# Sums of squares and state-space tables on VectorE alone, table builds one feature tile later, in a hybrid decoder layer

## The chip, the cores and the metric

One Trainium2 chip, one of its cores. The metric is the device time of one execution in microseconds (us); a result is the median of several executions.

## What is computed

One decoder layer over 512 tokens with 2048 features, in float32. The input is normalised, projected to q, k, v and u, goes through attention (q, k, v) and a diagonal state-space model (u) side by side, then through an output projection, a gated MLP and a last norm. Cut to what matters here:

```python
hn = _rmsnorm(h, norm1_g)                       # needs the sum of squares of each token
q, k, v, u = split(hn @ w_in)
a_bar = exp(lam * dt)                           # 64 groups x 64 complex states
b_bar = ((a_bar - 1.0) / lam)[..., None] * b_mat
bu = einsum('bsgp,gnp->bsgn', u, b_bar)
states = associative_scan(a, a * x + bu)        # over the 512 positions
y = einsum('bsgn,gpn->bsgp', states, c_mat).real + d_skip * u
ssm_out = gelu(y) * sigmoid(gelu(y) @ w_glu + b_glu)
h = h + concat([attn_out, ssm_out]) @ w_out
h = h + (silu(n(h) @ w_gate) * (n(h) @ w_up)) @ w_down
```

## The kernel before

Activations are kept transposed: features on the 128 partitions, tokens on the free axis. The projections are done at float32 accuracy by three matmuls on TensorE (PE) for each 128x128 block of weights and 128x512 block of activations: high by high, high by low, low by high (`mm3`, L108 to L111). So each weight chunk of 512 KB that arrives by DMA is split (`split`, L89 to L91): ScalarE (ACT) copies it into the high part, `whi`, and VectorE (DVE) subtracts to get the low part, `wlo`. There are four raw chunks and five pairs of high and low halves. Each of the 16 tiles of x is split the same way when it arrives (`gsplit`, whose VectorE half is the instruction at L59).

The program text gives instructions in program order, and a scheduler that simulates the engines then sets the order on each engine. Every engine works its own list strictly in that order, so an instruction whose input is late holds up all that stand behind it on that engine.

The stages, in the order of the program:

- **The x phase** (L198 to L222): x arrives in 16 tiles, is split, and tiles 0 and 1 of u are computed together, as the tiles arrive: 192 matmuls.
- **Sums of squares** (L223 to L230): ScalarE squares each tile of x into `sq_x`, and 15 additions gather them in `ssacc`, all on GpSimd (POOL) at L229. `rstd_of` (L141 to L161) turns them into the factor of the norm by small matmuls (`ss`, L146).
- **Tables** (L236 to L357): the powers `pr`, `pi` of the state matrix are computed on VectorE in many small operations, and the discretised input matrix `bbr`, `bbi` by six operations of 128x1024 (L330 to L335), three of them on GpSimd.
- **The u loop** (L451 to L458): tiles 2 to 7 of u (96 matmuls each). Behind a tile two of the eight `ssm_build` calls follow (tiles 3 to 6), and two of the eight `ssm_local` calls (tiles 4 to 7, the last one behind the first tile of q).
- **`ssm_build`** (L379 to L418): `combine` (L367 to L375) forms the table `E` of 128x1024 out of `bbr`, `bbi` and the powers: two products and a sum, in two halves of 512 columns, the first half on VectorE, the second on GpSimd. `cc` and `cz` (L392 to L394) are three small operations on GpSimd. TensorE transposes E in eight pieces (`etp`, L401) and multiplies it by `cz` (`gps`, L406); a DMA round trip turns the result into the table `T`.
- **`ssm_local`** (L422 to L438): products `vps` (L430) of u with E, copied to `Xh`, and `lps` (L437) with T.
- **The recurrence** (L482 to L489): 62 steps of five small VectorE operations on `Xh`, beside the tiles of q and k.
- **`ssm_out`** (L502 to L525): eight calls behind the tiles 5 to 7 of k. Each loads its part of Xh (`xt`, L509), forms a table `w` by `combine`, multiplies (`yps`, L517), adds to U on VectorE, applies Gelu on ScalarE and stores it by eight DMAs that ScalarE's queue issues (`sy`, L523).
- v (L542 to L554), attention, the gate of the state-space output, the output projection, and the MLP, which takes the rest of the time from about 770 us on.

Of the kernel before, what the change touches and what calls it, by code (L numbers as in the profile page):

```python
# [15 lines left out]
ALU = mybir.AluOpType  # L16
# [10 lines left out]
T = 8  # L27
# [8 lines left out]
def _emit(tc, a, y):  # L36
    nc = tc.nc
    act, dve, pool, pe = nc.scalar, nc.vector, nc.gpsimd, nc.tensor
# [10 lines left out]
    def tt(out, in0, in1, op, eng=None):  # L49
        (eng or dve).tensor_tensor(out=out, in0=in0, in1=in1, op=op)  # L50
# [33 lines left out]
    def aux(shape, name):  # L84
        return psum.tile(shape, F32, tag="aux", name=name, bufs=3)
# [55 lines left out]
    def rstd_of(acc_t, out, name):  # L141

        n = acc_t.shape[-1] // 128
        ps = aux([128, 4], "ss_" + name)
        for m in range(n):
            pe.matmul(ps[:, m:m + 1], acc_t[:, 128 * m:128 * m + 128], ones[:, 0:1], start=True, stop=True)  # L146
        st = cpool.tile([128, 4, 4], F32, tag="rst", name="rst_" + name)
        v, q, r, c = (st[:, i, :n] for i in range(4))
        ts(v, ps[:, :n], 1.0 / D, EPS, ALU.mult, ALU.add)
        act.activation(q, v, AF.Sqrt)  # L150
        dve.reciprocal(r, q)
        stt(q, v, -0.5, r, ALU.mult, ALU.mult)
        tt(q, q, r, ALU.mult)
        stt(c, q, 1.5, r, ALU.add, ALU.mult)
        dg = wpool.tile([128, 4, 128], F32, tag="sq", name="dg_" + name, bufs=4)
        for m in range(n):
            ts(dg[:, m, :], ident, c[:, m:m + 1])
        bc = aux([128, 512], "bc_" + name)
        pe.matmul(bc[:, :128 * n], ones, dg[:, :n].rearrange("p m t -> p (m t)"), start=True, stop=True)
        act.activation(out, bc[:, :128 * n], AF.Copy)  # L160
        return c  # L161
# [13 lines left out]
    ssacc = cpool.tile([128, 512], F32, tag="ss", name="ssacc")  # L175
# [47 lines left out]
    for k in range(KT):  # L223
        if k == 0:
            act.activation(ssacc, xr[k], AF.Square)
        else:
            sq = wpool.tile([128, 512], F32, tag="sq", name=f"sq_x{k}", bufs=4)
            act.activation(sq, xr[k], AF.Square)
            tt(ssacc, ssacc, sq, ALU.add, pool)  # L229
    rsc = rstd_of(ssacc, rstd, "1")  # L230

    for t, n in ((g2, "g2"), (gf, "gf"), (bg, "bg")):
# [15 lines left out]
    brt = sa.tile([128, NG, 16], F32, tag="E", name="brt")  # L248
    bit = sa.tile([128, NG, 16], F32, tag="tm", name="bit")
# [4 lines left out]
    z, k_, r, ki = small(), small(), small(), small().bitcast(I32)  # L254
# [42 lines left out]
    for n in (1, 2, 4):  # L297
# [4 lines left out]
        t_ = pt[:, :, :n]  # L302
# [23 lines left out]
    bbi = sp.tile([128, NG, 16], F32, name="bbi")  # L326
    bt = sp.tile([128, NG, 16], F32, tag="T", name="bt", bufs=2)
    frb = fr.unsqueeze(2).to_broadcast([128, NG, 16])
    fib = fi.unsqueeze(2).to_broadcast([128, NG, 16])
    tt(bbr, brt, frb, ALU.mult)  # L330
    tt(bbi, bit, frb, ALU.mult, pool)
    tt(bt, bit, fib, ALU.mult)
    tt(brt, brt, fib, ALU.mult, pool)
    tt(bbr, bbr, bt, ALU.subtract)
    tt(bbi, bbi, brt, ALU.add, pool)  # L335


    low, high = slice(0, 64), slice(64, 128)
# [2 lines left out]
    q4 = sp.tile([128, 2, NG], F32, name="q4")  # L341
# [24 lines left out]

    def combine(dst, tmp, c_re, c_im, n0):  # L367

        for i, eng in enumerate((dve, pool)):
            gs = slice(4 * i, 4 * i + 4)  # L370
            w = [c[:, gs].unsqueeze(2).to_broadcast([128, 4, T, 16]) for c in (c_re, c_im)]
            p = [t_[:, gs, n0:n0 + T].unsqueeze(3).to_broadcast([128, 4, T, 16]) for t_ in tables]
            tt(dst[:, gs], w[0], p[0], ALU.mult, eng)
            tt(tmp[:, gs], w[1], p[1], ALU.mult, eng)
            tt(dst[:, gs], dst[:, gs], tmp[:, gs], ALU.add, eng)  # L375

    built = {}

    def ssm_build(b):  # L379
        nonlocal tables  # L380
        gs = slice(8 * b, 8 * b + 8)
        tables = PA[:, gs], PB[:, gs]
        E_ = sa.tile([128, 8, T, 16], F32, tag="E", name=f"E{b}")
        tmp = sa.tile([128, 8, T, 16], F32, tag="tm", name=f"Et{b}")
        combine(E_, tmp, bbr[:, gs], bbi[:, gs], 0)

        cz = sp.tile([128, 8, 2, 16], F32, tag="cz", name=f"cz{b}", bufs=1)
        cc = sp.tile([128, 2, 8, 16], F32, tag="cb", name=f"cb{b}", bufs=1)
        side.dma_start(cc, a["c_c"][b])
        for r, pp in enumerate((slice(0, 64), slice(64, 128))):  # L390
            side.dma_start(cz[pp, :, 0], a["c_c"][b][pp, r])
        for r in range(2):  # L392
            tt(cc[:, r], cc[:, r], q4[:, r, gs].unsqueeze(2).to_broadcast([128, 8, 16]), ALU.mult, pool)
        tt(cz[:, :, 1], cc[:, 0], cc[:, 1], ALU.add, pool)  # L394
        dsk = sp.tile([16, 16, 8], F32, tag="dsk", name=f"dsk{b}", bufs=2)
        side.dma_start(dsk, a["d_skip"][:, :, 8 * b:8 * b + 8])
        et = sp.tile([128, 8, 128], F32, tag="et", name=f"et{b}", bufs=2)
        for i in range(2):
            ps = aux([128, 4, 128], f"etp{b}_{i}")
            for q in range(4):  # L400
                pe.transpose(ps[:, q, :], E_[:, 4 * i + q].rearrange("p a b -> p (a b)"), ident)  # L401
            act.activation(et[:, 4 * i:4 * i + 4], ps, AF.Copy)

        gps = aux([64, 8, 32], f"gps{b}")
        for q in range(8):
            pe.matmul(gps[:, q, :], E_[:, q, 0:4, :].rearrange("p a b -> p (a b)"), cz[:, q].rearrange("p a b -> p (a b)"),  # L406
                      start=True, stop=True)
        G = sp.tile([64, 2, 16, 8], F32, tag="G", name=f"G{b}", bufs=2)
        for i in range(2):
            act.activation(G[:, i], gps[:, :, 16 * i:16 * i + 16].rearrange("p g q -> p q g"), AF.Copy)  # L410
        tt(G[0:16, 0], G[0:16, 0], dsk, ALU.add)
        g_ = gz[b % 2]
        side.dma_start(g_[112:240].rearrange("(i r) q g -> r i (q g)", i=2), G.rearrange("p i q g -> p i (q g)"))
        tm_ = sp.tile([128, T, 16, 8], F32, tag="T", name=f"T{b}", bufs=2)
        src = g_[0:128].rearrange("r q g -> r (q g)")
        src = bass.AP(tensor=src.tensor, offset=src.offset, ap=[[128, 128], [16 * 128, T], [1, 128]])
        side.dma_start(tm_.rearrange("r i q g -> r i (q g)"), src)
        built[b] = et, tm_  # L418

    tables = None  # L420

    def ssm_local(b):  # L422
        p0, p1 = 4 * b, 4 * b + 4
        et, tm_ = built.pop(b)

        vps = aux([128, 2, 4, 64], f"vps{b}")
        for ri in range(2):
            for q in range(4):
                for e in range(2):
                    pe.matmul(vps[64 * e:64 * e + 64, ri, q, :], et[:, 2 * q + e, 64 * ri:64 * ri + 64],  # L430
                              U[:, 8 * b + 2 * q + e, :], start=True, stop=True)
        for ri in range(2):
            dve.tensor_copy(Xh[:, ri, p0:p1, 1:64], vps[:, ri, :, 0:63])

        lps = aux([128, 8, 64], f"lps{b}")
        for g in range(8):
            pe.matmul(lps[:, g, :], tm_[:, :, :, g].rearrange("p i q -> p (i q)"), U[:, 8 * b + g, :], start=True, stop=True)  # L437
        act.activation(U[:, 8 * b:8 * b + 8, :], lps, AF.Copy)  # L438

    def u_out(f, ps):  # L440
        ut = wpool.tile([128, T, NC_], F32, tag="sq", name=f"ut{f}", bufs=4)
        tt(ut, ps.rearrange("p (c j) -> p j c", j=T), rstd.rearrange("p (c j) -> p j c", j=T), ALU.mult)
        su = tc.dram_tile([128, T, NC_], F32, name=f"su{f}")
        side.dma_start(su, ut)
        sv = su.rearrange("(g p) j c -> j p g c", p=16)
        for j in range(T):
            side.dma_start(U[16 * (7 - j):16 * (7 - j) + 16, 8 * f:8 * f + 8, :], sv[j])

    u_out(0, u01[0])
    u_out(1, u01[1])  # L450
    for f in range(2, 8):  # L451
        ps = acc(f"u{f}")
        ftile(ps, [a["w_u"][2 * f], a["w_u"][2 * f + 1]], xs, f"u{f}")
        u_out(f, ps)
        for b in {4: (0, 1), 5: (2, 3), 6: (4, 5), 7: (6,)}.get(f, ()):
            ssm_local(b)
        for b in {3: (0, 1), 4: (2, 3), 5: (4, 5), 6: (6, 7)}.get(f, ()):
            ssm_build(b)  # L458
    qpool = opened("q", bufs=1)
    rc = qpool.tile([32, 512], F32, name="rc")  # L460
    rs = qpool.tile([32, 512], F32, name="rs")
# [14 lines left out]
        return t_  # L476

    qs = [qk_tile("q", 0, qpool)]
    ssm_local(7)


    for c in range(1, 63):  # L482
# [75 lines left out]
    for b in range(8):  # L558
        yt = wpool.tile([128, 512], F32, tag="sq", name=f"yt{b}", bufs=4)
        nc.sync.dma_start(yt, sy[b].rearrange("p i c -> p (i c)"))  # L560
        t_ = laid(ring2, "B", f"ysp{b}", 8, 4)
# [23 lines left out]
    for h in range(NH):  # L585
# [4 lines left out]
        for step in "t0 t1 t2 p0 t3 p1 p2 p3".split():  # L590
            j = int(step[1])
            w = 512 - 128 * j
# [84 lines left out]
    for e in range(2):  # L677
        es = E[e]
        for f in range(KT):
# [9 lines left out]
            else:  # L689
                sq = wpool.tile([128, 512], F32, tag="sq", name=f"sq_h{e}_{f}", bufs=4)[:, 0:256]  # L690
# [112 lines left out]
    for p in range(NPH):  # L803
        ms = []
        for q in range(4):
            f = 4 * p + q
# [114 lines left out]
```

## Time and profile before

| | us |
|---|---|
| median of 3 runs | 2112.76 (2112.38 to 2114.86) |
| the profiled execution, its own time | 2112.28 |
| span of that execution in the profile | 2110.5 |
| TensorE busy | 2053.3 (97%) |
| VectorE busy | 1535.6 (73%) |
| ScalarE busy | 865.6 (41%) |
| GpSimd busy | 198.1 (9%) |
| mean granted TensorE clock | 0.986 |

The busy times are those of one execution. Its own time is 1.8 us over its span, since the span goes from the first to the last instruction. The mean clock is a share of full speed (2.4 GHz); the two levels that are granted are 1.2 and 2.4 GHz. Matmuls overlap, so the time from one start to the next says more about TensorE's pace than the duration of one.

### The profile page before, as it was taken

To read this page: it belongs to the slowest core of one execution; us is meant where nothing else is said; L and a number is where in the kernel's file an instruction comes from. 1 tells how busy PE (TensorE), PEld (TensorE's weight loads), DVE (VectorE), ACT (ScalarE), POOL (GpSimd) and SP (SyncE) were. 2 spreads that over 40 slices of the span, in tenths; PEclk is the share of its full clock that TensorE was granted. 3 is DMA by queue.
4 is the path that set the end of the run, shared out by engine and by line. 5 is a ranking of instruction groups with operands and counts; after the bars stand their busy time and mean duration, and the time that the engine had idled before them with its cause. 6 is when DMAs were issued, how large, how long until landed. Compare 5 with 4: busy or idle time off the path is not lost.

```text
span 2110.5 us, 35164 instructions
## 1 busy us (share of the span) xinstructions
PE 2053.3 (97%) x13522; PEld 1858.4 (88%) x13522; DVE 1535.6 (73%) x2932; ACT 865.6 (41%) x1523; POOL 198.1 (9%) x172
## 2 busy tenths in 40 slices
PE   7899999999999979999999999999999999999996
PEld 5688888877889979899998989899998989999896
DVE  8835897555436989687786968687686868778686
ACT  5222222346325645344443535344352535444354
POOL 4533102300002360000000000000000000000002
PEclk9999999999999989999999999999999999999998
DMA  6443234623324614323232223323232332323232
GB/s 222 127 121 112 92 102 140 178 81 125 125 91 169 206 65 140 121 100 120 82 129 90 101 101 120 111 90 130 85 124 83 111 110 101 120 88 124 90 121 80
DMA packets 117193, 244.24 MB, mean 116 GB/s; under 512 B 39040, under 2 KB 57312, under 8 KB 117024
## 3 DMA queue, kind: packets, MB, share of 16 engines
q1 hardware_dynamic: 107808, 239.88, 33.8%
q10 hardware_dynamic: 9216, 2.10, 0.5%
q8 instruction: 106, 1.74, 0.3%
q14 instruction: 63, 0.52, 0.1%
HBM read 229.77 MB, written 9.03 MB: 113 GB/s over the span
## 4 chain that ended last, share of the span: by engine, by line
PE 87%; DVE 7%; issue 2%; DMA 1%; ACT 1%; SPq 0%; POOL 0%; DVEq 0%; ACTq 0%; POOLq 0%
PE gu L109 12%; PE gu L111 12%; PE gu L110 12%; PE dn L110 7%; PE dn L109 7%; PE dn L111 7%; PE lps L437 1%; PE q L111 1%; PE q L110 1%; PE oa L111 1%; PE oa L109 1%; PE oa L110 1%; PE q L109 1%; PE v L550 1%; PE v L552 1%
## 5 line engine op out<-in xcount | busy, mean ns | idle before, releaser
L110 PE MATMUL dn<-m,whi_dn 128*128 128x512 f32 x640 | 249.0, 389 | 0.0
L109 PE MATMUL dn<-m,whi_dn 128*128 128x512 f32 x640 | 248.8, 389 | 0.0
L111 PE MATMUL dn<-m,wlo_dn 128*128 128x512 f32 x640 | 248.8, 389 | 0.0
L50 DVE TENSOR_TENSOR h<-h,dn 128x512 f32<-128x512 f32 x160 | 109.9, 687 | 172.5 <-PE dn L111 171.3
L90 ACT ACTIVATE whi_dn<-raw_dn 128x512 fp32r<-128x512 f32 x160 | 100.9, 632 | 240.5 <-PE dn L110 208.2
L50 DVE TENSOR_TENSOR raw_r<-raw_r,raw_r 128x512 f32<-128x512 f32 x264 | 182.5, 691 | 2.2
L111 PEld LDWEIGHTS dn<-m,wlo_dn 128*128 128x128 f32 x640 | 120.2, 188 | 24.9
L109 PEld LDWEIGHTS dn<-m,whi_dn 128*128 128x128 f32 x640 | 120.2, 188 | 24.6
L110 PEld LDWEIGHTS dn<-m,whi_dn 128*128 128x128 f32 x640 | 120.2, 188 | 24.5
L50 POOL TENSOR_TENSOR h<-h,ssf 128x256 f32<-128x256 f32 x12 | 10.7, 920 | 1300.1 <-ACT ssf L160 1300.1
L50 DVE TENSOR_TENSOR wlo_dn<-raw_dn,whi_dn 128x512 fp32r<-128x512 f32 x160 | 109.8, 687 | 17.6 <-ACT whi_dn L90 16.5
L109 PE MATMUL gu<-c,whi_C 128*128 128x256 f32 x352 | 99.8, 284 | 1.9 <-ACT c L90 1.6
L111 PE MATMUL gu<-c,wlo_E 128*128 128x256 f32 x352 | 98.8, 281 | 2.8 <-DVE wlo_E L50 2.8
L109 PE MATMUL gu<-c,whi_D 128*128 128x256 f32 x352 | 98.3, 279 | 2.7 <-ACT whi_D L90 2.7
L109 PE MATMUL gu<-c,whi_E 128*128 128x256 f32 x352 | 98.5, 280 | 2.4 <-ACT whi_G L90 1.7
L111 PE MATMUL gu<-c,wlo_D 128*128 128x256 f32 x352 | 98.5, 280 | 2.0 <-DVE wlo_D L50 2.0
L111 PE MATMUL gu<-c,wlo_C 128*128 128x256 f32 x352 | 99.5, 283 | 0.5 <-DVE wlo_C L50 0.5
L110 PE MATMUL gu<-c,whi_C 128*128 128x256 f32 x352 | 99.6, 283 | 0.1
L110 PE MATMUL gu<-c,whi_E 128*128 128x256 f32 x352 | 98.3, 279 | 0.0
L110 PE MATMUL gu<-c,whi_D 128*128 128x256 f32 x352 | 98.0, 278 | 0.0
L109 PE MATMUL gu<-c,whi_F 128*128 128x256 f32 x352 | 97.7, 277 | 0.0
L109 PE MATMUL gu<-c,whi_G 128*128 128x256 f32 x352 | 97.5, 277 | 0.2 <-ACT whi_G L90 0.2
(323 smaller groups left out, 6673.1 us busy)
## 6 DMA issues: line engine op xcount, KB each, us to landing
raw_r<-w_gu SPq DMA_DIRECT2D x176, 512.0 KB, 3.6
raw_dn<-w_down SPq DMA_DIRECT2D x80, 512.0 KB, 4.1
raw_os<-w_out SPq DMA_DIRECT2D x32, 512.0 KB, 3.4
raw_q<-w_q SPq DMA_DIRECT2D x16, 512.0 KB, 3.5
raw_k<-w_k SPq DMA_DIRECT2D x16, 512.0 KB, 3.4
raw_v<-w_v SPq DMA_DIRECT2D x16, 512.0 KB, 3.7
raw_oa<-w_out SPq DMA_DIRECT2D x16, 512.0 KB, 3.5
raw_u<-w_u SPq DMA_DIRECT2D x15, 512.0 KB, 4.7
```

What stands on the lines that cost most here:

```text
L50: (eng or dve).tensor_tensor(out=out, in0=in0, in1=in1, op=op)
L90: act.activation(hi, raw, AF.Copy)
L109: pe.matmul(ps, wh, x[:, 0, :], start=first, stop=False)
L110: pe.matmul(ps, wh, x[:, 1, :], start=False, stop=False)
L111: pe.matmul(ps, wl, x[:, 0, :], start=False, stop=last)
L437: pe.matmul(lps[:, g, :], tm_[:, :, :, g].rearrange("p i q -> p (i q)"), U[:, 8 * b + g, :], start=True, stop=True)
L550: pe.matmul(pss[m], xs[kt][:, 0, ms], wh, start=kt == 0, stop=False)
L552: pe.matmul(pss[m], xs[kt][:, 1, ms], wh, start=False, stop=kt == 15)
```

## The change

All that GpSimd did in the sums of squares, in `bbi`, in `combine`, and in `cc` and `cz` is given to VectorE. `combine` now makes three operations of 128x1024 in place of three of 128x512 on each of the two engines. And the builds and locals of the state-space tables come one tile of u later: builds behind tiles 4 to 7 in place of 3 to 6, locals behind tiles 5 to 7 and the first tile of q.

```diff
--- before.py
+++ after.py
@@ -226,7 +226,7 @@
         else:
             sq = wpool.tile([128, 512], F32, tag="sq", name=f"sq_x{k}", bufs=4)
             act.activation(sq, xr[k], AF.Square)
-            tt(ssacc, ssacc, sq, ALU.add, pool)
+            tt(ssacc, ssacc, sq, ALU.add)
     rsc = rstd_of(ssacc, rstd, "1")
 
     for t, n in ((g2, "g2"), (gf, "gf"), (bg, "bg")):
@@ -328,11 +328,11 @@
     frb = fr.unsqueeze(2).to_broadcast([128, NG, 16])
     fib = fi.unsqueeze(2).to_broadcast([128, NG, 16])
     tt(bbr, brt, frb, ALU.mult)
-    tt(bbi, bit, frb, ALU.mult, pool)
+    tt(bbi, bit, frb, ALU.mult)
     tt(bt, bit, fib, ALU.mult)
-    tt(brt, brt, fib, ALU.mult, pool)
+    tt(brt, brt, fib, ALU.mult)
     tt(bbr, bbr, bt, ALU.subtract)
-    tt(bbi, bbi, brt, ALU.add, pool)
+    tt(bbi, bbi, brt, ALU.add)
 
 
     low, high = slice(0, 64), slice(64, 128)
@@ -366,13 +366,11 @@
 
     def combine(dst, tmp, c_re, c_im, n0):
 
-        for i, eng in enumerate((dve, pool)):
-            gs = slice(4 * i, 4 * i + 4)
-            w = [c[:, gs].unsqueeze(2).to_broadcast([128, 4, T, 16]) for c in (c_re, c_im)]
-            p = [t_[:, gs, n0:n0 + T].unsqueeze(3).to_broadcast([128, 4, T, 16]) for t_ in tables]
-            tt(dst[:, gs], w[0], p[0], ALU.mult, eng)
-            tt(tmp[:, gs], w[1], p[1], ALU.mult, eng)
-            tt(dst[:, gs], dst[:, gs], tmp[:, gs], ALU.add, eng)
+        w = [c.unsqueeze(2).to_broadcast([128, 8, T, 16]) for c in (c_re, c_im)]
+        p = [t_[:, :, n0:n0 + T].unsqueeze(3).to_broadcast([128, 8, T, 16]) for t_ in tables]
+        tt(dst, w[0], p[0], ALU.mult)
+        tt(tmp, w[1], p[1], ALU.mult)
+        tt(dst, dst, tmp, ALU.add)
 
     built = {}
 
@@ -390,8 +388,8 @@
         for r, pp in enumerate((slice(0, 64), slice(64, 128))):
             side.dma_start(cz[pp, :, 0], a["c_c"][b][pp, r])
         for r in range(2):
-            tt(cc[:, r], cc[:, r], q4[:, r, gs].unsqueeze(2).to_broadcast([128, 8, 16]), ALU.mult, pool)
-        tt(cz[:, :, 1], cc[:, 0], cc[:, 1], ALU.add, pool)
+            tt(cc[:, r], cc[:, r], q4[:, r, gs].unsqueeze(2).to_broadcast([128, 8, 16]), ALU.mult)
+        tt(cz[:, :, 1], cc[:, 0], cc[:, 1], ALU.add)
         dsk = sp.tile([16, 16, 8], F32, tag="dsk", name=f"dsk{b}", bufs=2)
         side.dma_start(dsk, a["d_skip"][:, :, 8 * b:8 * b + 8])
         et = sp.tile([128, 8, 128], F32, tag="et", name=f"et{b}", bufs=2)
@@ -446,16 +444,20 @@
         for j in range(T):
             side.dma_start(U[16 * (7 - j):16 * (7 - j) + 16, 8 * f:8 * f + 8, :], sv[j])
 
+    def ssm_step(f):
+
+        for b in {5: (0, 1), 6: (2, 3), 7: (4, 5), 8: (6, 7)}.get(f, ()):
+            ssm_local(b)
+        for b in {4: (0, 1), 5: (2, 3), 6: (4, 5), 7: (6, 7)}.get(f, ()):
+            ssm_build(b)
+
     u_out(0, u01[0])
     u_out(1, u01[1])
     for f in range(2, 8):
         ps = acc(f"u{f}")
         ftile(ps, [a["w_u"][2 * f], a["w_u"][2 * f + 1]], xs, f"u{f}")
         u_out(f, ps)
-        for b in {4: (0, 1), 5: (2, 3), 6: (4, 5), 7: (6,)}.get(f, ()):
-            ssm_local(b)
-        for b in {3: (0, 1), 4: (2, 3), 5: (4, 5), 6: (6, 7)}.get(f, ()):
-            ssm_build(b)
+        ssm_step(f)
     qpool = opened("q", bufs=1)
     rc = qpool.tile([32, 512], F32, name="rc")
     rs = qpool.tile([32, 512], F32, name="rs")
@@ -476,7 +478,7 @@
         return t_
 
     qs = [qk_tile("q", 0, qpool)]
-    ssm_local(7)
+    ssm_step(8)
 
 
     for c in range(1, 63):
```

Line numbers of the changed kernel are 2 larger behind `combine` until the u loop (`etp` L399, `gps` L404: 2 smaller) and 2 larger behind the loop (`yps` L519).

The order on the engines moves too. VectorE in the x phase, as a piece of the difference (`x8` and so on are the low halves of x's tiles, `wlo_u1_1_0` that of a weight chunk of u's tile 1):

```order
 L59 SCALAR_TENSOR_TENSOR x8_201<-Xh_83,g1_66,x8_201 128x512
 L59 SCALAR_TENSOR_TENSOR x9_204<-Xh_83,g1_66,x9_204 128x512
+L50 TENSOR_TENSOR ssacc_78<-ssacc_78,sq_x8_308 128x512
 L50 TENSOR_TENSOR wlo_u1_1_0_210<-raw_u1_1_207,whi_u1_1_0_209 128x512
 L59 SCALAR_TENSOR_TENSOR x10_218<-Xh_83,g1_66,x10_218 128x512
+L50 TENSOR_TENSOR ssacc_78<-ssacc_78,sq_x9_311 128x512
 L50 TENSOR_TENSOR scr_T_358<-scr_T_358 128x64
 L59 SCALAR_TENSOR_TENSOR x11_221<-Xh_83,g1_66,x11_221 128x512
```

The additions that GpSimd made now stand between the splits of x's tiles: eight of them between the splits of tiles 4 and 15, and four more behind.

TensorE at the first build, before (`u4` is a tile of u, `etp0` and `gps0` belong to the first build):

```order
L109 MATMUL u4_766<-x15_235,whi_u4_1_1_807 128x512
L110 MATMUL u4_766<-x15_235,whi_u4_1_1_807 128x512
L111 MATMUL u4_766<-x15_235,wlo_u4_1_1_808 128x512
L401 MATMUL etp0_0_691<-ident_70,E0_672 128x128 x4
L401 MATMUL etp0_1_697<-ident_70,E0_672 128x128 x4
L406 MATMUL gps0_703<-cz0_680,E0_672 64x32 x8
```

and now:

```order
L110 MATMUL u6_1068<-x4_129,whi_u6_0_1_1075 128x512
L111 MATMUL u6_1068<-x4_129,wlo_u6_0_1_1076 128x512
L109 MATMUL u6_1068<-x5_132,whi_u6_0_1_1075 128x512
L399 MATMUL etp0_0_769<-ident_70,E0_753 128x128 x4
L399 MATMUL etp0_1_775<-ident_70,E0_753 128x128 x4
L404 MATMUL gps0_781<-cz0_758,E0_753 64x32 x8
```

240 matmuls of the projections stood ahead of the first transpose; 304 do now.

TensorE at the end of `ssm_out`, before (`v0_1` and so on are accumulators of v, `yps7` the last product of the state-space output):

```order
L551 MATMUL v0_1_3585<-wlo_v0_6_0_3795,x12_225 128x512
L552 MATMUL v0_1_3585<-whi_v0_6_0_3794,x12_225 128x512
L517 MATMUL yps7_3546<-xt7_3533,w7_3538 128x64 x8
L550 MATMUL v0_2_3586<-whi_v0_6_0_3794,x12_225 128x512
L551 MATMUL v0_2_3586<-wlo_v0_6_0_3795,x12_225 128x512
```

and now (`sc0_0` is the first product of attention):

```order
L554 MATMUL v1_0_3816<-whi_v1_1_1_3860,x3_125 128x512
L519 MATMUL yps6_3466<-xt6_3456,w6_3461 128x64 x8
L552 MATMUL v1_0_3816<-whi_v1_2_0_3890,x4_129 128x512
L553 MATMUL v1_0_3816<-wlo_v1_2_0_3891,x4_129 128x512
L554 MATMUL v1_0_3816<-whi_v1_2_0_3890,x4_129 128x512
L519 MATMUL yps7_3498<-xt7_3488,w7_3493 128x64 x8
L576 MATMUL sc0_0_4140<-kh0_2715,qh0_1598 128x128
```

The last product has moved from the first half of v into the second, and it stands three matmuls behind the one before it, where 31 to 48 stood between two of them before.

## Rows read from the trace of the kernel before

**Rows 1.** Busy time by stretch; the first line names the columns.

```profile
core 0: us, PE busy (x) PEld busy (x) DVE busy (x) ACT busy (x) POOL busy (x), PEclk, DMA share, GB/s
25.00:50.00 25.00, 20.73 (x80) 16.23 (x81) 24.25 (x62) 8.61 (x16) 11.59 (x9) 0.86 0.58 164
41.50:87.25 45.75, 36.92 (x164) 29.72 (x162) 42.26 (x109) 12.41 (x20) 16.68 (x9) 0.97 0.33 101
100.00:150.00 50.00, 50.00 (x361) 43.90 (x360) 20.30 (x31) 11.51 (x24) 20.39 (x20) 0.97 0.53 143
770.00:780.00 10.00, 6.73 (x29) 6.23 (x30) 10.00 (x14) 4.92 (x10) 5.92 (x6) 0.53 0.00 0
```

**Rows 2.** TensorE's waits, 0 to 700 us: who waits for whom: total us, times, longest.

```profile
PE etp L401 <- DVE E L50: 6.3, 1, 6.3
...
PE u L110 <- DVE x L59: 5.7, 3, 2.8
PE u L111 <- DVE wlo_u L50: 2.6, 1, 2.6
```

**Rows 3.** Timeline, VectorE, 25 to 90 us: start, us, what, count.

```profile
29.17 1.77 DVE L59 SCALAR_TENSOR_TENSOR x<-Xh,g,x 128x512 fp32r<-128x512 f32 x1
...
40.19 0.74 DVE L59 SCALAR_TENSOR_TENSOR x<-Xh,g,x 128x512 fp32r<-128x512 f32 x1
...
41.50 0.69 DVE L50 TENSOR_TENSOR wlo_u<-raw_u,whi_u 128x512 fp32r<-128x512 f32 x1
...
58.67 1.24 DVE L50 TENSOR_TENSOR bbr<-brt,scr_T 128x1024 f32<-128x1024 f32 x1
...
64.95 3.41 DVE L50 TENSOR_TENSOR bt<-bit,scr_et 128x1024 f32<-128x1024 f32 x1
```

**Rows 4.** Timeline, GpSimd, 5 to 70 us.

```profile
8.58 1.32 POOL L50 TENSOR_TENSOR ssacc<-ssacc,sq_x 128x512 f32<-128x512 f32 x1 [7.75 <-ACT sq_x L228]
13.82 23.17 POOL L50 TENSOR_TENSOR ssacc<-ssacc,sq_x 128x512 f32<-128x512 f32 x14 [3.92 <-ACT sq_x L228]
...
58.31 4.49 POOL L50 TENSOR_TENSOR bbi<-bit,scr_T 128x1024 f32<-128x1024 f32 x1 [21.17 <-DVE scr_T L50]
```

**Rows 5.** Timeline, TensorE, 20 to 50 us.

```profile
23.16 0.39 PE L109 MATMUL u<-x,whi_u 128*128 128x512 f32 x1
...
48.51 0.95 PE L146 MATMUL ss<-ones,ssacc 128*128 128x1 f32 x8
```

**Rows 6.** Timeline, TensorE, 84 to 104 us: the first build.

```profile
87.30 1.97 PE L401 MATMUL etp<-ident,E 128*128 128x128 f32 x8 [6.32 <-DVE E L50]
89.20 1.92 PE L406 MATMUL gps<-cz,E 128*64 128x32 f32 x16
91.05 0.80 PE L109 MATMUL u<-x,whi_u 128*128 128x512 f32 x1
...
95.39 0.39 PE L111 MATMUL u<-x,wlo_u 128*128 128x512 f32 x1
...
98.59 0.39 PE L110 MATMUL u<-x,whi_u 128*128 128x512 f32 x1
98.82 0.60 PE L401 MATMUL etp<-ident,E 128*128 128x128 f32 x4
...
102.09 1.06 PE L406 MATMUL gps<-cz,E 128*64 128x32 f32 x15
```

**Rows 7.** Timeline, TensorE: the last `vps` and the first `yps`.

```profile
201.76 1.98 PE L430 MATMUL vps<-U,et 128*64 128x64 f32 x32
...
336.85 1.89 PE L517 MATMUL yps<-xt,w 128*128 128x64 f32 x16
```

**Rows 8.** Timeline, VectorE: the recurrence's last step.

```profile
328.64 0.29 DVE L50 TENSOR_TENSOR Xh<-Xh,m 128x64 f32<-128x64 f32 x1
```

**Rows 9.** The 32 transfers of L509, `xt`: from issue to landing.

```profile
DMA to landing us min/median/max: 1.9/2.1/3.6
```

**Rows 10.** Timeline, ScalarE's queue: the stores of one `ssm_out`.

```profile
340.48 4.86 ACTq L523 DMA_DIRECT2D sy<-U  x8
```

## The prediction

> **What bounds the kernel now.** I read the page first: TensorE is busy for 2053.3 us of 2110.5 (97%), so the time is TensorE's list plus what TensorE loses, and work that leaves GpSimd (9% busy) is worth nothing by itself. So I looked for TensorE's losses next, in its waits and in the busy time by stretch. From 100 to 150 us TensorE is busy for all of 50.00 us [rows 1], with the builds running on VectorE and GpSimd beside it. The losses that this change can touch lie earlier: 6.3 us in one wait of the first transposes for E, 5.7 us for low halves of x, 2.6 us for one `wlo` of u [rows 2]. All three are waits for VectorE, and VectorE is busy for 24.25 of the 25 us from 25 to 50 [rows 1]. That, and not TensorE, is what bounds the start.
>
> Why is VectorE so slow there? The reader is to see that one and the same instruction takes 1.77 us at 29.17 and 0.74 us at 40.19 [rows 3]. In between GpSimd's additions stop: they run from 13.82 for 23.17 us [rows 4]. Likewise `bt` takes 3.41 us and `bbr`, of the same shape, 1.24 [rows 3]; `bt` runs while GpSimd makes its 128x1024 operations, which begin at 58.31 [rows 4]. So two-input operations of VectorE and GpSimd's own stretch each other. The 14 additions take 23.17 us, 1.655 us each; a VectorE subtraction takes 0.69 undisturbed [rows 3], which leaves about 0.97 us that each addition costs VectorE when both have work.
>
> The Trainium skill ("SBUF — State Buffer", section "Who interferes with whom") says that a VectorE instruction with two inputs in SBUF contends with a GpSimd instruction that reads there, and that the loser blocks for the whole instruction. By that an addition would cost VectorE its full 1.32 us [rows 4], 18.5 us for 14 instead of 13.6, and the trace, with 0.97, agrees only in part. Since TensorE's own pace limits the gain in this phase, the sum below would be the same.
>
> **The change, part by part.** All terms stand against the profiled execution, 2112.28 us.
>
> 1. *The x phase.* TensorE's pace undisturbed is 14 starts from 95.39 to 98.59, 0.229 us each [rows 6]. From 23.16 to the `ss` products at 48.51 [rows 5] its list holds 70 large matmuls, 16.0 us; it takes 25.35. So 9.3 us are lost, the waits for x among them. In the changed order VectorE has, from the fifth tile of x to the last, 12 splits at 0.74, 8 additions at 0.69, 4 `wlo` at 0.69 and about 1 us of small operations [rows 3]: 18.2 us, or some 16.5 as the starts overlap. Three further additions stand ahead (2.1 us, part of it in idle time). With the start near 16 the last split ends between 32.5 and 34.5, where it now ends at 40.93 [rows 3]. TensorE at full pace asks for that tile 42 matmuls behind 23.16, at 32.8. So VectorE is late by 0 to 1.7 us: a gain of 7.6 to 9.3; I take 8.5. If the additions cost more than their bare duration, 6 is the lower end. **-8.5** (-6 to -9.3).
> 2. *The `wlo` wait.* It has the same cause [rows 2]. **-2.6** (0 to -2.6).
> 3. *The first E.* The wait is 6.3 us, and TensorE comes out of it at half its clock: 8 transposes take 1.97 us where 4 take 0.60 later, 16 `gps` 1.92 where 15 take 1.06, and 11 starts of matmuls 4.34 us (91.05 to 95.39) instead of 2.5 [rows 6]. Together that is 3.5 us; the two make 9.8. With the delay TensorE comes to the first transposes after 304 matmuls: from 118 at 48.51 less 8.5, which is 40.0, another 186 by 0.229 gives 82.6, and about 1 us of small products 83.6. When is E ready? Between 41.50 and 87.25 VectorE is busy for 42.26 us [rows 1]. To that stretch the change adds 7 operations of 512 columns (4.8), 6 of 1024 (7.4) and some 2 us of small ones, 14.2; it takes away the stretching by GpSimd's 9 instructions [rows 1] at 0.97, 8.7. So 48 us without idle time, 51 with the same idle time, from about 34: E is ready between 82 and 85, and TensorE waits 0 to 2 us. I take 1. **-9.8 and +1**. If the stretching doesn't go, the whole 9.8 is lost again.
> 4. *Recurrence to the first `yps`.* It is all on VectorE and untouched, but starts a tile later in relation to TensorE. From the last `vps` to the first `yps` 135.1 us pass now [rows 7], for 563 matmuls; in the new order there are 553, 2.3 us less: 132.8. The recurrence ends at 328.93 [rows 8], 127.2 behind that `vps`; the four transfers of `xt` are issued within some 2 us and take 2.1 to land, at most 3.6 [rows 9], which makes 131.3 to 132.8. The slack of 3.8 us shrinks to between 0 and 1.5. **+0.5** (0 to +5, the latter with a restart at half clock like that of step 3).
> 5. *The end of v.* The last two `yps` now stand three matmuls apart (0.7 us). Between them VectorE must add to U (0.69) and make two operations of 1024 for w7 (1.24 each) [rows 3], 3.2 us: a wait of 2.5. Behind the last one ScalarE issues eight stores for 4.86 us [rows 10] ahead of the copies out of v's accumulators; I estimate that 1.8 of it reaches TensorE. With a part of the 3.5 us of a restart I take **+5** (0 to +8).
> 6. *Other builds and `ssm_out`.* A `combine` of three operations at 1.24 is 1.65 us longer on VectorE than three at 0.69; from 100 to 150 VectorE is busy for 20.30 of 50 us [rows 1], which hides it. GpSimd's queue gets empty and nobody waits for it. **0**. In the early MLP, where VectorE is full and TensorE is busy for 6.73 of 10 us [rows 1], a reshuffled list can win or lose up to 3 us; **0** (-3 to +3).
>
> Sum: -8.5 - 2.6 - 9.8 + 1 + 0.5 + 5 = -14.4, so 2097.9. The median of the runs stands 0.5 above the profiled execution: **2098 us**.
>
> **The rivals.**
>
> *A: the late state-space work gives more back.* Steps 4 and 5 at their upper ends: TensorE waits at the first `yps` and restarts at half clock (+5 in place of +0.5), and the end of v costs 8 instead of 5. For it: a slack of under 2 us. Against it: other work of VectorE fills the gaps of the recurrence, and that may be ordered better as well. 2098 + 4.5 + 3 = 2106.
>
> *B: slower, VectorE is simply full.* If the long rows are not GpSimd's doing but, say, that of the arriving x, moving the additions only lengthens VectorE's list: 11 additions at 0.69 ahead of the last split put it 7.6 us later, and TensorE with it; E comes 7.6 + 14.2 later, at 109, where TensorE now asks at 95.6 + 7.6 = 103.2 (81.0 before the wait, plus 64 matmuls): a wait of 5.8 instead of 6.3. With steps 4 and 5: +7.6 - 0.5 + 5.5 = 12.6, so 2125. It decides from the point where the last split of x ends after 40.93. Against it stands the subtraction at 41.50, back at 0.69 with the additions over [rows 3, 4]. The Trainium skill ("Perfetto Trace Analysis", section "Optimizing Scalar/DVE Operations") says that with VectorE saturated, offloading to GpSimd may make sense, which speaks for this rival; it adds that the two share a read port, so that it might not help. The rows above side with the addition.
>
> *C: no change.* The gain of the x phase appears, but E is as late as before, since VectorE's list until E is 14.2 us longer, and the end takes its 8: -8.5 - 2.6 + 0 + 0.5 + 8 = -2.6, so 2110. For it: step 3 rests on a difference of two large numbers.
>
> *D: more.* Steps 4 and 5 at 0 and step 1 at 9.3, or a better MLP order: 2098 - 5.5 - 0.8 - 3 = 2089.
>
> **How the numbers follow.** A measurement of this kernel can tell about 0.2%, 4.2 us, from no change: faster is below 2108.5, slower above 2117. Forecast 0.60, A 0.20, C 0.08, B 0.06, D 0.06. Faster: forecast, A and D, 0.86; same: C, 0.08; slower: B, 0.06. The range reaches from 2090 (D nearly whole) to 2108 (A and 2 us of the unknown in step 3); B, C and the tail of D are left out.
>
> **What would show it.** Right: no VectorE row of 512 columns near 1.7 us before 100 us; additions at 0.69 between the splits; `ss`'s neighbours on TensorE at about 40 us; no wait of `etp` over 2 us and no half clock behind it; 100 to 150 us as full as now. Steps 4 and 5 show as new waits of `yps` for `xt` and for w7. Wrong: splits of x at 1.7 us with GpSimd idle (B), a wait of several us for E (C), or new losses in the stretches from 330 to 430 us.

## The result and the profile after

| | before | changed |
|---|---|---|
| median of 4 runs, us | 2113.51 (2112.38 to 2114.86) | 2098.64 (2097.72 to 2100.22) |
| ratio | | 0.9921 (0.9908 to 0.9933) |
| the profiled execution, us | 2112.28 | 2100.22 |
| its span, us | 2110.5 | 2098.4 |
| TensorE busy | 2053.3 | 2053.3 (98%) |
| VectorE busy | 1535.6 | 1533.5 (73%) |
| GpSimd busy | 198.1 | 74.6 (4%) |

The change makes the kernel 14.9 us faster by the medians, 12.1 by the two spans; the forecast was 2098. The two measures differ since the profiled execution of the changed kernel is the slowest of its four, and that of the kernel before lies below all of its runs. VectorE took over all that GpSimd did here and is not busier for it.

The busy time by stretch of the changed kernel, columns as in [rows 1]:

```profile
25.00:50.00 25.00, 25.00 (x116) 20.87 (x115) 23.13 (x83) 14.83 (x26) 0.20 (x1) 1.00 0.68 207
75.00:100.00 25.00, 24.21 (x163) 19.97 (x162) 17.87 (x28) 7.27 (x15) 0.00 (x0) 1.00 0.73 204
95.00:240.00 145.00, 144.85 (x909) 125.08 (x910) 80.10 (x172) 34.49 (x67) 0.00 (x0) 0.93 0.39 109
...
400.00:405.00 5.00, 2.53 (x19) 2.08 (x19) 3.74 (x4) 0.63 (x1) 0.00 (x0) 1.00 0.13 23
405.00:410.00 5.00, 5.00 (x25) 4.47 (x25) 0.69 (x1) 2.94 (x5) 0.00 (x0) 0.66 0.39 88
```

From 25 to 50 us TensorE is now busy all the time and at full clock (before 20.73 of 25 us at 0.86). Two rows are worse than before: the granted clock from 95 to 240 us, 0.93, and TensorE's 2.5 idle us at 400, with half clock behind.

The same window of the kernel before, where the clock is 0.96:

```profile
95.00:240.00 145.00, 145.00 (x933) 125.23 (x932) 77.18 (x164) 36.59 (x70) 46.69 (x41) 0.96 0.41 119
```

VectorE's timeline, the rows that answer to [rows 3] (the last split of x is that of 31.20):

```profile
23.66 0.69 DVE L50 TENSOR_TENSOR ssacc<-ssacc,sq_x 128x512 f32<-128x512 f32 x1
...
24.86 0.75 DVE L59 SCALAR_TENSOR_TENSOR x<-Xh,g,x 128x512 fp32r<-128x512 f32 x1
...
31.20 0.75 DVE L59 SCALAR_TENSOR_TENSOR x<-Xh,g,x 128x512 fp32r<-128x512 f32 x1
...
63.38 1.22 DVE L50 TENSOR_TENSOR bt<-bit,scr_et 128x1024 f32<-128x1024 f32 x1
...
80.88 1.22 DVE L50 TENSOR_TENSOR E<-E,Et 128x1024 f32<-128x1024 f32 x1
```

The stretched rows are gone: splits take 0.75 us beside the additions at 0.69, `bt` 1.22 instead of 3.41. The last split ends at 31.95 instead of 40.93, and the first E is ready at 82.10 instead of 87.25, although VectorE now makes all of it.

TensorE's timeline at the first build, and the row that answers to `ss` of [rows 5]:

```profile
44.70 0.95 PE L146 MATMUL ss<-ones,ssacc 128*128 128x1 f32 x8
...
83.91 1.04 PE L399 MATMUL etp<-ident,E 128*128 128x128 f32 x8
84.87 1.12 PE L404 MATMUL gps<-cz,E 128*64 128x32 f32 x16
```

TensorE asks for E at 83.91, 1.8 us behind its being ready: no wait and full clock (1.04 us for the eight transposes, 1.97 in [rows 6]). `ss` stands behind 139 large matmuls now, 118 before. Counted by large matmuls (the 128x512 ones), the start of the 118th, the last one ahead of the old place of `ss`, has come 8.6 us forward (48.28 to 39.71), and that of the 220th, behind the old wait for `wlo`, 11.4.

Where the rest goes is seen by two landmarks that stand behind the same work in both kernels: the last matmul of q (all builds and locals are done) and the last of v. The answers on these tiles, before:

```profile
L111 PE MATMUL q<-x,wlo_q x128: 389/389/628, 154.6 to 271.3; 128*128 128x512 f32 x128
L552 PE MATMUL v<-whi_v,x x128: 387/389/476, 364.6 to 461.4; 128*128 128x512 f32 x128
```

and after:

```profile
L111 PE MATMUL q<-x,wlo_q x128: 387/389/796, 122.5 to 255.1; 128*128 128x512 f32 x128
L554 PE MATMUL v<-whi_v,x x128: 387/389/628, 344.7 to 449.5; 128*128 128x512 f32 x128
```

(the last number is the start of the last one.) At the end of q the change is 16.2 us ahead, at the end of v 11.9, and from there to the end 1649.1 us pass before and 1648.9 after: attention, gate and MLP contribute nothing.

The loss of 4.3 us between the two lies at the last two products of the state-space output. TensorE's timeline there:

```profile
399.82 1.73 PE L519 MATMUL yps<-xt,w 128*128 128x64 f32 x14
...
404.77 2.22 PE L519 MATMUL yps<-xt,w 128*128 128x64 f32 x16 [2.47 <-issue]
```

and VectorE's:

```profile
401.59 0.69 DVE L50 TENSOR_TENSOR U<-yps,U 128x512 f32<-128x512 f32 x1 [0.87 <-PE yps L519]
402.20 1.22 DVE L50 TENSOR_TENSOR w<-cc,pr 128x1024 f32<-128x1024 f32 x1
403.45 1.23 DVE L50 TENSOR_TENSOR w<-w,wt 128x1024 f32<-128x1024 f32 x1
```

VectorE makes w7 only when the product for w6 has released its one buffer; TensorE waits 2.47 us, until 0.1 us behind the end of w7 (404.68). The profile puts the wait down to "issue", the rows of VectorE explain it. The other input of the last product, `xt`, is there in time: its loads are issued by 395.4 and land at most 3.9 us later.

```profile
L511 SPq DMA_DIRECT2D xt<-Xh x32: 467/592/1488, 335.0 to 395.4; - x32
DMA to landing us min/median/max: 1.9/2.2/3.9
```

### The profile page after: what moved, and what is told of

Its sections match the earlier page's. It is cut to its first block, busy times and chain, and to the rows that moved or that the text cites. A ratio compares the mean times of both kernels' runs of the same rounds, so it can differ in the third digit from the quotient of the medians.

```text
span 2098.4 us, 35067 instructions
## 1 busy us (share of the span) xinstructions
PE 2053.3 (98%) x13522; PEld 1859.9 (89%) x13522; DVE 1533.5 (73%) x2974; ACT 865.5 (41%) x1523; POOL 74.6 (4%) x82
## 3 DMA queue, kind: packets, MB, share of 16 engines
q8 instruction: 106, 1.74, 0.3%
## 4 chain that ended last, share of the span: by engine, by line
PE 91%; DVE 5%; issue 2%; ACT 1%; DMA 1%; POOL 0%; SPq 0%; DVEq 0%; ACTq 0%; POOLq 0%
PE gu L109 13%; PE gu L111 13%; PE gu L110 12%; PE dn L110 7%; PE dn L109 7%; PE dn L111 7%; PE q L111 1%; PE q L110 1%; PE u L109 1%; PE u L110 1%; PE lps L435 1%; PE q L109 1%; PE u L111 1%; PE oa L109 1%; PE oa L111 1%
## 5 line engine op out<-in xcount | busy, mean ns | idle before, releaser
L50 DVE TENSOR_TENSOR wlo_dn<-raw_dn,whi_dn 128x512 fp32r<-128x512 f32 x160 | 109.8, 687 | 17.2 <-ACT whi_dn L90 16.2
L109 PE MATMUL gu<-c,whi_F 128*128 128x256 f32 x352 | 97.9, 278 | 0.0
L110 PE MATMUL gu<-c,whi_F 128*128 128x256 f32 x352 | 97.9, 278 | 0.0
L111 PE MATMUL gu<-c,wlo_F 128*128 128x256 f32 x352 | 97.7, 278 | 0.0
```

The source lines that it names most:

```text
L109: pe.matmul(ps, wh, x[:, 0, :], start=first, stop=False)
L110: pe.matmul(ps, wh, x[:, 1, :], start=False, stop=False)
L111: pe.matmul(ps, wl, x[:, 0, :], start=False, stop=last)
```

## The experiments

What each run gave is put as its median and ratio to the kernel before on the same chip, and as landmarks of its profile: the start of the last matmul of q and of v, and the span. The medians of the kernel before were 2116.9, 2113.9 and 2117.5 us in the three series, so times of different series are compared by ratio or span. A span is that of one execution, and the one profile of the kernel before (2110.5) serves for all series. The sums alone, the tables alone, no delay and the idle additions ran in the first series, the last three rows in the third.

| run | median us | ratio (95%) | end of q | q to v | span |
|---|---|---|---|---|---|
| before | | | 271.3 | 190.1 | 2110.5 |
| changed | 2098.64 | 0.9921 (0.9908 to 0.9933) | 255.1 | 194.4 | 2098.4 |
| sums alone | 2099.19 | 0.9908 (0.9888 to 0.9929) | 258.4 | 190.2 | 2098.5 |
| tables alone | 2108.94 | 0.9962 (0.9946 to 0.9978) | 267.1 | 193.8 | 2109.4 |
| no delay | 2099.23 | 0.9909 (0.9888 to 0.9931) | 253.6 | 196.0 | 2098.1 |
| idle additions | 2109.97 | 0.9961 (0.9945 to 0.9978) | 263.4 | 194.5 | 2107.0 |
| idle fills | 2100.61 (one run) | | 255.1 | 194.4 | 2098.8 |
| two buffers for w | 2094.56 | 0.9906 (0.9892 to 0.9921) | 253.7 | 191.4 | 2093.6 |
| w in halves | 2095.79 | 0.9915 (0.9898 to 0.9931) | 251.8 | 192.1 | 2092.5 |
| apart | 2091.97 | 0.9898 (0.9883 to 0.9913) | 252.3 | 190.0 | 2089.9 |
| changed, again | 2100.16 | 0.9916 (0.9899 to 0.9934) | 252.3 | 194.5 | 2094.1 |
| apart, again | 2092.70 | 0.9883 (0.9867 to 0.9899) | 253.0 | 190.1 | 2091.2 |
| apart, w in halves | 2093.90 | 0.9893 (0.9875 to 0.9912) | 252.6 | 190.1 | 2091.4 |

### Which part of the change does it

Theory A: GpSimd's two-input work stretches VectorE's, and VectorE bounds the start. Rivals: B, VectorE is merely full; L, the later builds are what counts.

**The sums alone**, in the kernel before:

```diff
-            tt(ssacc, ssacc, sq, ALU.add, pool)
+            tt(ssacc, ssacc, sq, ALU.add)
```

> Only the 15 additions of the sums of squares go to VectorE; tables, combine and the builds' place stay as before. Theory A (GpSimd's two-input work stretches VectorE's, and VectorE bounds the start): the x phase gains 8.5 us and the wait for wlo 2.6; E is ready at about 85 us while TensorE asks at about 76, so that wait grows from 6.3 to some 9 us: 2105 us (2102 to 2109). Rival B (VectorE is merely full, its long rows are not GpSimd's doing): the last split of x ends later than 40.9 us, 2115 us or more. Rival L (the later builds are what counts): no gain, 2113 us.

B and L fall: one word gives a span of 2098.5 us, as the whole change does, and the last split of x, for which B needed an end after 40.9, ends at 31.2. A is right in the direction, but its 2105 us was a miss. VectorE's rows of that split and of the end of E, then TensorE's timeline at the first build:

```profile
30.49 0.75 DVE L59 SCALAR_TENSOR_TENSOR x<-Xh,g,x 128x512 fp32r<-128x512 f32 x1
...
78.74 0.68 DVE L50 TENSOR_TENSOR E<-E,Et 128x512 f32<-128x512 f32 x1
```

```profile
79.47 1.97 PE L401 MATMUL etp<-ident,E 128*128 128x128 f32 x8 [3.57 <-DVE E L50]
81.37 1.92 PE L406 MATMUL gps<-cz,E 128*64 128x32 f32 x16
```

TensorE asks at 75.9, as expected; E is ready at 79.4, not at 85, so the wait shrinks to 3.6 us instead of growing to 9. The edit moves TensorE's order too: 271 large matmuls stand ahead of the first transposes here, 240 before. Without these 31 (7.0 us) the wait would have grown, to some 10 us by an estimate from these rows. Moving the additions brought E forward by 7.8 us, against 9.7 for the last split of x, which ends at 31.2 here: the additions behind it cost VectorE some 2 us, not the 6 that I had added. The restart at half clock is still there, and from q to v nothing is lost.

**The tables alone**: the changed kernel with the additions left on GpSimd.

```diff
-            tt(ssacc, ssacc, sq, ALU.add)
+            tt(ssacc, ssacc, sq, ALU.add, pool)
```

> The whole change but for the sums of squares, whose additions stay on GpSimd. Theory A: the x phase loses 9.3 us as before and the wait for wlo stays; TensorE asks for E at about 89 us, E is ready at about 87: no wait, 9.8 us gained; some 4 us are lost at the end of v: 2107 us (2103 to 2110). With the run of the sums alone, the two gains add up to that of the whole change within 3 us. A rival that puts E's wait down to the x phase alone: the wait of 6 us for E stays, 2113 us or more.

The runs, 0.9962, lie within the expectation; the profile shows less, a span 1.1 us under that of before. The wait for E is gone but for 0.4 us, as expected. The wait for `wlo`, expected to stay, is gone too: the 118th large matmul starts 1.6 us later than before, the 220th 1.2 us earlier. But at the end of q only 4.2 us are left, and 3.7 go at the end of v. Whether the parts add up depends on the measure. By spans they do: 12.0 and 1.1 make 13.1, against 12.1 for the whole. By the medians on this one chip they don't: the sums alone gain 17.7 us, the tables alone 8.0, and the whole change without the delay (next run) 17.7. By both, the tables add nothing to the sums alone.

**Without the delay**: the changed kernel with builds and locals at their old tiles.

```diff
-        for b in {5: (0, 1), 6: (2, 3), 7: (4, 5), 8: (6, 7)}.get(f, ()):
+        for b in {4: (0, 1), 5: (2, 3), 6: (4, 5), 7: (6,), 8: (7,)}.get(f, ()):
             ssm_local(b)
-        for b in {4: (0, 1), 5: (2, 3), 6: (4, 5), 7: (6, 7)}.get(f, ()):
+        for b in {3: (0, 1), 4: (2, 3), 5: (4, 5), 6: (6, 7)}.get(f, ()):
             ssm_build(b)
```

> The changed kernel with builds and locals back at their old tiles of u in the program text. The scheduler's order is the same on TensorE, ScalarE and GpSimd, and differs in 2 rows on VectorE and 5 on SP. Theory A: 2098.6 us as the whole change, within 2 us. Rival L (the delay is what spares TensorE the wait for E): a wait of over 5 us for E and a restart at half clock come back, 2108 us.

2099.2 us, a span of 2098.1: the delay is worth nothing. The first transposes stand behind 304 matmuls with it and without it. Presumably the scheduler puts them there because in its own simulation E comes later once VectorE makes all of it; no run tests that.

### What GpSimd costs VectorE

**Idle additions**: beside the x phase of the changed kernel, GpSimd works for nobody.

```diff
+    dum = cpool.tile([128, 512], F32, name="dum")
     for k in range(KT):
...
             tt(ssacc, ssacc, sq, ALU.add)
+            if k == 1:
+                tt(dum, sq, sq, ALU.mult, pool)
+            else:
+                tt(dum, dum, dum, ALU.add, pool)
```

> The changed kernel, and beside its x phase 15 two-input operations of 128x512 on GpSimd whose results nobody reads (the first reads one square, the others their own tile); the order on all other engines is that of the changed kernel. Theory A: each of them costs VectorE 0.97 us as in the kernel before, splits of x take 1.7 us again, the x phase and E are late by up to 13.6 us: 2111 us (2107 to 2114); by a lock for the whole instruction, 1.32 us each, 2116 us. Rival B: nothing changes, 2098 us, splits at 0.74 us.

This is the cleanest test of A: the lists of all other engines are those of the changed kernel. 2110 us, 10.7 over the run without the delay on the same chip; the span is 8.6 us over that of the changed kernel. VectorE's timeline beside the idle additions:

```profile
8.60 1.53 DVE L50 TENSOR_TENSOR ssacc<-ssacc,sq_x 128x512 f32<-128x512 f32 x1
...
15.31 2.97 DVE L59 SCALAR_TENSOR_TENSOR x<-U,g,x 128x512 fp32r<-128x512 f32 x2
18.20 2.97 DVE L50 TENSOR_TENSOR ssacc<-ssacc,sq_x 128x512 f32<-128x512 f32 x2
...
29.77 0.68 DVE L50 TENSOR_TENSOR ssacc<-ssacc,sq_x 128x512 f32<-128x512 f32 x1
```

and GpSimd's:

```profile
8.50 1.08 POOL L50 TENSOR_TENSOR dum<-sq_x 128x512 f32<-128x512 f32 x1 [7.67 <-ACT sq_x L229]
9.66 19.64 POOL L50 TENSOR_TENSOR dum<-dum 128x512 f32<-128x512 f32 x14
```

The two engines go in step, one instruction each: VectorE's pace is 1.45 us (two splits from 15.31 to 18.20), GpSimd's 1.40 (19.64 by 14), and at 29.3, where GpSimd ends, VectorE is back at 0.68. Undisturbed the pace of the splits is 0.66, so each costs 0.79 us, not the 0.97 of my estimate. What GpSimd takes undisturbed, this run doesn't show: its first row, 1.08, stands beside VectorE's stretched addition at 8.60. In the kernel before, a GpSimd addition of 128x512 takes 1.29 us while VectorE is idle:

```profile
130.04 1.29 POOL L50 TENSOR_TENSOR E<-E,Et 128x512 f32<-128x512 f32 x1
```

By the Trainium skill ("SBUF — State Buffer", section "Who interferes with whom") one would wait out the whole instruction of the other; I estimate a pair at 0.66 + 1.08 = 1.74 us, or 0.66 + 1.29 = 1.95, and 1.45 was measured. So the two instructions, as the profile times them, still overlap in part; whether the lock is shorter than the instruction or is shared, no run here shows.

**Idle fills**: the same, but 14 of the 15 operations only write.

```diff
-                tt(dum, dum, dum, ALU.add, pool)
+                pool.memset(dum, 0.0)
```

> As the run with the idle additions, but 14 of GpSimd's 15 operations only fill their tile (128x512, no input from SBUF). If it is GpSimd's reading that stretches VectorE (theory A), VectorE's splits stay at 0.74 us and the span at 2098.4 us (within 1.5). If any work of GpSimd does it, splits of up to 1.5 us and a span of 2102 us or more, as far as the fills last.

GpSimd's timeline, then VectorE's beside it:

```profile
10.15 8.11 POOL L234 MEMSET dum<- 128x512 f32 x14
```

```profile
12.73 1.42 DVE L59 SCALAR_TENSOR_TENSOR x<-U,g,x 128x512 fp32r<-128x512 f32 x2
14.06 1.49 DVE L50 TENSOR_TENSOR ssacc<-ssacc,sq_x 128x512 f32<-128x512 f32 x2
```

In the midst of the fills two splits take 1.42 us together, as undisturbed, and the span is 2098.8. So GpSimd's additions cost VectorE time and its fills don't: of what the two differ in, its reading is the likely cause, as expected. (The fills end at 18.3, so they cover only a part of the x phase.)

### The loss at the end of v

**Two buffers for w**, and **w in halves** on VectorE and GpSimd as before, both in the changed kernel (`halves` is the old `combine`):

```diff
-        w = sa.tile([128, 8, T, 16], F32, tag="E", name=f"w{b}")
+        w = sc_.tile([128, 8, T, 16], F32, tag="w", name=f"w{b}", bufs=2)
```

```diff
-        combine(w, tmp, cc[:, 0], cc[:, 1], 1)
+        halves(w, tmp, cc[:, 0], cc[:, 1], 1)
```

> The changed kernel with two buffers for the table w of the state-space output, so that w7 can be made while the product for w6 still waits. Theory A with step 5 of the prediction: the wait of 2.5 us ahead of the last product and the stretch at half clock behind it go, 4.3 us in all (16.2 us ahead of the kernel before at the end of q, 11.9 at the end of v): a span of 2094 us (2093 to 2096). Rival: the wait is put down to no semaphore by the profile; if it is the loads of xt, it stays and so does the time, 2098 us.

> The changed kernel, but the tables w of the state-space output are formed in two halves on VectorE and GpSimd as before; the last two products are 28 matmuls apart again. Theory A: no wait at the end of v, 4.3 us saved; but the first product stands 21 matmuls (4.8 us) earlier and may wait up to 3 us for the end of the recurrence: a span of 2094 to 2098 us. If VectorE stretched by GpSimd mattered here too, 2100 us or more.

The first came as expected, 2093.6 us of span; the second, 2092.5, is 1.5 under its range. With two buffers the wait is gone and q to v is 191.4 us long instead of 194.4. In halves it is 192.1, with new waits of 1.5 us for `xt`. Neither edit is a test of the buffer alone, since both move the products: with two buffers 1293 large matmuls stand ahead of the last one, 1359 in the changed kernel. The rival, the loads of xt, falls by the rows of the change above. So w made whole by VectorE, in one buffer, was the losing part of the change.

### The clock behind the locals

The granted clock of 0.93 from 95 to 240 us needs its own test. TensorE's timeline behind the first two locals of the changed kernel:

```profile
98.59 1.15 PE L428 MATMUL vps<-U,et 128*64 128x64 f32 x32
99.84 4.04 PE L435 MATMUL lps<-U,T 128*128 128x64 f32 x16
103.81 1.98 PE L428 MATMUL vps<-U,et 128*64 128x64 f32 x32
...
107.16 0.63 PE L110 MATMUL u<-x,whi_u 128*128 128x512 f32 x1
107.59 0.63 PE L111 MATMUL u<-x,wlo_u 128*128 128x512 f32 x1
...
110.96 0.39 PE L110 MATMUL u<-x,whi_u 128*128 128x512 f32 x1
111.19 0.40 PE L111 MATMUL u<-x,wlo_u 128*128 128x512 f32 x1
```

The large matmuls start 0.43 us apart (1.2 GHz) until 109, then 0.23 (2.4 GHz). From 98.59 TensorE has had only small products, without a gap over 0.1 us, and the second `vps`, with 1.98 us where the first takes 1.15, is at the lower clock already. Three of the four pairs of locals show it in this profile. The kernel before shows it behind its first pair too (matmuls of 0.63 us from 110.29 on), but the same sequence of its second pair stays at full clock:

```profile
141.11 1.15 PE L430 MATMUL vps<-U,et 128*64 128x64 f32 x32
...
142.78 0.40 PE L109 MATMUL u<-x,whi_u 128*128 128x512 f32 x1
143.01 0.40 PE L110 MATMUL u<-x,whi_u 128*128 128x512 f32 x1
```

**Apart**: one build and one local behind each half of a tile of u; only the last two locals stay together, behind the first tile of q. The edit, cut:

```diff
...
+            if c and mid:
+                mid()
...
-        ftile(ps, [a["w_u"][2 * f], a["w_u"][2 * f + 1]], xs, f"u{f}")
+        ftile(ps, [a["w_u"][2 * f], a["w_u"][2 * f + 1]], xs, f"u{f}", lambda: ssm_step(f - 1, 1))
         u_out(f, ps)
-        ssm_step(f)
+        ssm_step(f, 0)
```

> The changed kernel with one build and one local behind each half of a tile of u instead of two behind each tile; in the scheduler's order the two locals of a pair stand 21 to 42 large matmuls apart, and the last two products of the output 31. If the stretches at half clock from 100 to 220 us come from two locals one behind the other, they go: 3.7 us saved, and 4.3 us at the end of v: a span of 2090.5 us (2089 to 2093). If the clock falls behind single locals too, 2094 us.

2089.9 us of span, as the first theory said, but not by its mechanism. The loss at the end of v is gone (q to v 190.0), since the last two products stand 34 large matmuls apart in this order. The locals of a pair stand only 14 to 16 large matmuls apart in the trace, not the 21 to 42 of the expectation, and those of the last pair 0. The clock is hardly better, here beside the sums alone (from 95 to 240 us; apart, then sums alone):

```profile
95.00:240.00 145.00, 144.64 (x904) 124.47 (x903) 93.99 (x246) 34.48 (x65) 0.00 (x0) 0.94 0.41 112
```

```profile
95.00:240.00 145.00, 145.00 (x913) 125.25 (x910) 84.86 (x186) 36.38 (x68) 44.39 (x39) 0.94 0.41 121
```

So three more kernels ran on one chip: the changed one, the same, and both mends together.

> The changed kernel once more, for what its own runs differ by: five runs with its order up to the end of q stood 11.4 to 13.3 us ahead of the kernel before ahead of the first build, and 16.2 to 19.5 at the end of q. A span of 2098 us (2095 to 2099); the 4.3 us at the end of v are lost again.

> Builds and locals one behind each half tile, once more, beside the changed kernel on the same chip. If its gain is that of the end of v alone (the first run's profile still shows half clock behind single locals): 4.3 us under the changed kernel, 0.2%. If spacing helps the clock too, 8 us, 0.4%.

> Builds and locals one behind each half tile, and the tables w in two halves on VectorE and GpSimd. As neither order shows a wait at the end of v, the two mends are the same one: the time of the kernel with builds and locals apart, within 2 us. If they add up, 4 us less.

The changed kernel's span is 2094.1 us this time, with the same order and below the expected 2095 to 2099: the end of q comes 2.8 us sooner. Of these, 1.2 us are there ahead of the first build already (the transposes start at 82.72, in the first profile at 83.91); the other 1.6 come behind it, at a clock of 0.95:

```profile
95.00:240.00 145.00, 144.48 (x905) 124.48 (x906) 82.19 (x183) 35.06 (x67) 0.00 (x0) 0.95 0.41 113
```

The loss at the end of v is the same (194.5 from q to v). So 2 to 3 us of difference up to q are between executions, and single profiles don't settle less. "Apart" again gains its 4.4 us from q to v; its end of q, 253.0, is within what the changed kernel itself shows. The medians, 2092.7 and 2100.2, differ by 7.5 us, more than the 2.9 of these two spans; the runs of the changed kernel scatter over 5.6 us (2095.9 to 2101.5). So whether spacing gains more than the 4.4 stays open. The two mends don't add up (2091.4), as expected. "Apart" has the lowest ratios of the study, 0.9898 and 0.9883, against 0.9921 and 0.9916 for the change; on the last chip its slowest run, 2093.8, is under the fastest of the change, 2095.9.

What makes the clock fall behind some small products and not behind others stays open.

## Why the prediction was right

The number was right, 2098 against 2098.6, and most terms were right by themselves. One term was missing, half clock behind the locals, 5.0 us in the profiled execution. The six others came out 0.1 to 1.0 us better than forecast, 2.7 together, which made up half of it; by the two spans the gain is 12.1 us where the sum had 14.4. That the median lies within 0.6 us is in part luck: the four runs of the change spread over 2.5 us.

1. *The x phase*: -8.5 forecast, 8.6 us measured at the 118th matmul in the profile of the change, 8.9 to 10.5 in the other runs with its order up to the end of q (idle additions aside). The last split ends at 31.95, forecast 32.5 to 34.5. The cause is shown: GpSimd working for nobody brings the loss back, at 0.79 us for each VectorE instruction beside it; the 118th matmul then starts 1.6 us later than in the kernel before.
2. *The `wlo` wait*: -2.6 forecast; the gain grows by 2.8, from 8.6 to 11.4, across its place, and it is no longer among the waits. That it has "the same cause" as the loss of the x phase holds only in the wide sense of GpSimd stretching VectorE: it also goes with the tables alone, where the additions stay on GpSimd. Probably what goes there is the stretching of rows such as `bt` (3.41 us before, 1.24 in that run).
3. *The first E*: forecast ready between 82 and 85 and asked for at 83.6; ready at 82.1, asked for at 83.9. The wait and the restart are gone. Three things were wrong here. "With the delay TensorE comes to the first transposes after 304 matmuls": the delay has no part in it, as the run without it shows. The 1 us of waiting didn't come. And the sum had no term for half clock later on: behind the 240th large matmul 9.8 us should be gained up to the end of q, and 4.8 are (190.8 us before, 186.0 now), so 5.0 are lost. Between 95 and 240 us the granted clock is 0.93 instead of the 0.96 that the same window shows for the kernel before, 4.4 us of full clock; that is most of the 5.0, as far as one profile can say. The second profile of the change, at 0.95, loses 3.4.
4. *The first `yps`*: +0.5 forecast, no wait measured.
5. *The end of v*: +5 forecast, 4.3 measured; a wait of 2.5 forecast, 2.47 measured, and half clock behind it. That ScalarE's stores hold up v's copies was not seen as a term of its own.
6. *MLP*: 0 forecast, 0.2 us measured.

Of the rivals, A would have needed a loss of 13 us behind q, D none; 4.3 were measured. B fell with the sums alone and C with E ready at 82.1. What the prediction didn't see is the division: it gave the additions and the tables shares of some 8 and 6 us (in the expectations), where one word at the additions gives 12 of 12 by spans and the rest of the change as much as it takes. With w left in halves or with two buffers the span is 5 to 6 us under that of the sums alone, of which up to 3 may be differences between executions; the ratios, 0.9915 and 0.9906 against 0.9908, show no difference. So that the tables pay on top of the sums is not shown.

## What to carry to other kernels

Before giving work to an idle engine, look whether the busy one gets longer rows while the idle one works: the same instruction at two durations in one timeline is the sign, and a run in which the idle engine works for nobody is the proof. Split a change into its parts even when the forecast fits: here one line gave as much as the whole, one part gave nothing, and one lost 4 us, of which 3 came back with a second buffer. Where a scheduler sets the order, see in the order whether an edit moves anything at all.

## What was not expected of the hardware

Two-input instructions of VectorE and GpSimd of 128x512 ran in step, one for one, at 1.45 and 1.40 us, where VectorE's pace alone is 0.66 and an undisturbed GpSimd addition took 1.29: dearer than side by side and cheaper than one after the other. GpSimd's fills, 0.58 us each, cost VectorE nothing. And with the same order TensorE's clock from 95 to 240 us was granted at 0.93 in one execution and 0.95 in another; between the first build and the end of q the second was 1.6 us shorter.
